# Two layers of a trunk in one launch: weights first at the start, b and k swapped in one head's half, five transposes a pair, samples behind the last chain

## The chip, the cores and the metric

One core of one Trainium2 chip runs the whole program. The metric is the device time of one execution in microseconds (us); a profile of one execution stands beside it.

## The reference

One inference step of a two-layer trunk, model width 1024, over 256 prompt tokens and 8 samples of 4 tokens, 288 columns in all, in float32. Layer 0 mixes tokens with Mamba-2, layer 1 with RWKV-7; around the mixers stand SwiGLU blocks and a gated table product, at the end a norm:

```
for i in range(2):
    h += 0.5 * swiglu(rmsnorm(h), ffn1[i])
    h += mamba2(rmsnorm(h)) if i == 0 else rwkv7(rmsnorm(h))
    h += 0.5 * swiglu(rmsnorm(h), ffn2[i])
    h += (p[i] @ ple_in[i]) * sigmoid(rmsnorm(h) @ ple_gate[i])
y = rmsnorm(h)
```

The change concerns RWKV-7 above all. For each of 16 heads of 64 features, with r, k, v, decay d, a unit vector kk and a gate a, it carries a 64x64 state:

```
sa = S @ -kk_t
S  = S * d_t + sa (kk_t * a_t)^T + v_t k_t^T
y_t = S @ r_t
```

The prompt starts from zero; each of the 8 samples has a state of its own, which is an output. y is then normalised per head, a bonus sum(r * k * r_k) * v is added, the result is gated and multiplied by w_o.

## The kernel before

Features lie on partitions (eight tiles `h[k]` of 128x288), tokens on the free axis. The stages run in the order above. Weights come as a stream of 512 KB units of eight 128x128 tiles (`Stream.load`, L46, on SyncE's queue). ScalarE copies each half unit into a rounded part `whi` (L61) and VectorE subtracts to get the rest `wlo` (L62); a product is three matmuls of 288 columns (L160, L161, L162).

`start` (L243 to L247) issues the vectors `vec`, two tiles of h, the first weight unit, and six tiles of h, all from SyncE. Meanwhile `prologue` (L441) runs WARM = 16 rounds of matmuls on a constant tile. `final` sums squares over features with six matmuls (L419: three for `ss`, three for `sq`), transposes the result 24 times into token rows (L429), scales each block of 512 columns by the norm on ScalarE or VectorE (L434) and stores it (L435).

The RWKV stage takes heads in pairs: `p` counts eight of them, and the two heads of a pair are the two halves of the 128 partitions. Per pair there are these parts:

- `bulk` and `bulk2`: the projections, matmuls of 128x288. They are the filler that a loop weaves in between the others, RATE = 1.6 of its steps for each round of the chains.
- `prep` (from L1260): the decay E1, its inverse E2, and the tiles `AR` (kk and r, scaled) and `BK` (b = kk times a in slot 0, k in slot 1, both times E2), each holding four chunks of 64 prompt tokens and one with the samples. `pad_mul` (L1255 the chunks, L1257 the samples) writes them on VectorE. `by_tokens` multiplies BK with AR (masked into `AA`, L1313 and L1322) and, against an identity, turns BK into `BKt` with tokens on partitions; all of it is L1307. After it comes a triangular inverse by small matmuls (L1352).
- `chain` (from L1410): chunk by chunk `solve` (L1435 to L1444), `solved` (L1449, L1450) and `state` (L1461 to L1469); in chunk 2 the samples: `masked` builds `SVm` (L1479), `samples` multiplies (L1486, L1489), updates the sample states `S0` on VectorE (L1491, L1492) and stores them. Then center (L1233 and L1234, a matrix that subtracts the mean), squares, `ones_m` for the variance, and the gated output.
- `wo`: the output products, filler of the last pairs. EARLY output tiles are taken in hand one round sooner; TAIL tells how many steps fill each round behind the last chain.

A scheduler sets the order on each engine; only in the tail the order written is kept (`k.keep`).

## Time and profile before

| What | Value |
| --- | --- |
| Runs | 1524.62, 1524.87, 1526.18 us; median 1524.87 |
| Profiled execution | 1526.08 us, span 1524.3 us |
| Busy TensorE, VectorE, ScalarE, GpSimd | 1503.7, 1107.9, 971.8, 62.0 us |
| RWKV, head pairs | about 1000 to 1260 us |
| One head pair in the middle | 30.6 us, TensorE busy 30.41 |
| First real matmul | at 7.90 us |

The profile is of one execution. Times are in microseconds, PE is TensorE (PEld its weight load), DVE VectorE, ACT ScalarE, POOL GpSimd, SP SyncE; a q behind the name is the engine's queue. L12 is line 12 of the kernel before. A group row gives busy time, mean ns of one, and the idle time ahead of the engine with what ended it; a row of the timeline gives start, length, and in brackets that idle time.

### The profile page before, as it was taken

What the parts mean: (1) busy time and instruction counts of PE and PEld (TensorE: products, weight loads), DVE (VectorE), ACT (ScalarE), POOL (GpSimd) and SP (SyncE); (2) the same over time, 40 slices, a digit from 0 to 9 for tenths busy, and PEclk for the clock granted to TensorE, in tenths of its full rate; (3) what the DMA queues carried; (4) which work ended last, traced back from release to release, by engine and by line L of the source; (5) the groups of instructions that cost most, each with busy time, mean ns of one, the idle gap of its engine ahead of it and who ended that gap; (6) DMA issues with size and microseconds to landing.
All of it is one profiled execution on the core that took longest, in us unless ns stands there. A gap on an engine that the chain in (4) does not pass through costs nothing.

```text
span 1524.3 us, 35699 instructions
## 1 busy us (share of the span) xinstructions
PE 1503.7 (99%) x14210; PEld 1425.9 (94%) x14210; DVE 1107.9 (73%) x2336; ACT 971.8 (64%) x2217; POOL 62.0 (4%) x162
## 2 busy tenths in 40 slices
PE   9999999999999999999999999999999999999997
PEld 9999999999999999999999999778887779999997
DVE  7666568899998766656866655898888768666566
ACT  6555458999997655554755554687767646555545
POOL 0000002112110000000000000300000000000000
PEclk9999999999999999999999999999999999999999
DMA  7555564766766555555555555612222225555552
GB/s 232 166 166 167 167 203 141 236 237 217 235 224 192 180 167 166 166 166 167 161 168 166 167 167 166 207 69 73 85 72 83 74 66 169 167 167 166 166 169 67
DMA packets 75575, 243.48 MB, mean 160 GB/s; under 512 B 11728, under 2 KB 16976, under 8 KB 75408
## 3 DMA queue, kind: packets, MB, share of 16 engines
q1 hardware_dynamic: 75408, 241.21, 50.2%
q8 instruction: 111, 1.82, 0.5%
q14 instruction: 56, 0.46, 0.1%
HBM read 226.54 MB, written 14.64 MB: 158 GB/s over the span
## 4 chain that ended last, share of the span: by engine, by line
PE 90%; DVE 4%; ACT 3%; DMA 1%; issue 1%; SPq 0%; DVEq 0%; ACTq 0%
PE bank L160 25%; PE bank L162 25%; PE bank L161 25%; PE bank L1352 2%; PE bank L1307 1%; PE bank L785 1%; DVE wlo L62 1%; PE bank L1172 1%; PE bank L789 1%; PE bank L781 1%; PE bank L1489 1%; PE bank L1461 1%; PE bank L1449 1%; PE bank L1421 1%; DMA raw<-in_w 1%
## 5 line engine op out<-in xcount | busy, mean ns | idle before, releaser
L160 PE MATMUL bank<-act,whi 128*128 128x288 f32 x2792 | 833.5, 299 | 2.3 <-ACT whi L61 0.8
L161 PE MATMUL bank<-act,whi 128*128 128x288 f32 x2792 | 828.8, 297 | 0.0
L162 PE MATMUL bank<-act,wlo 128*128 128x288 f32 x2792 | 824.7, 296 | 0.1
L61 ACT ACTIVATE whi<-raw 128x512 fp32r<-128x512 f32 x762 | 478.3, 632 | 438.1 <-PE bank L161 425.5
L62 DVE TENSOR_TENSOR wlo<-raw,whi 128x512 fp32r<-128x512 f32 x762 | 521.5, 690 | 269.8 <-ACT whi L61 241.3
L162 PEld LDWEIGHTS bank<-act,wlo 128*128 128x128 f32 x2792 | 527.6, 189 | 5.0 <-issue 2.4
L161 PEld LDWEIGHTS bank<-act,whi 128*128 128x128 f32 x2792 | 528.5, 189 | 3.7 <-DVE act L172 0.3
L160 PEld LDWEIGHTS bank<-act,whi 128*128 128x128 f32 x2792 | 524.1, 188 | 7.8 <-ACT whi L61 1.3
L160 PE MATMUL bank<-more,whi 128*128 128x288 f32 x192 | 56.7, 296 | 0.0
L337 DVE TENSOR_TENSOR u<-bank,s 128x288 f32<-128x288 f32 x88 | 40.2, 457 | 22.8 <-PE bank L162 22.8
L161 PE MATMUL bank<-more,whi 128*128 128x288 f32 x192 | 56.5, 294 | 0.0
L162 PE MATMUL bank<-more,wlo 128*128 128x288 f32 x192 | 56.4, 294 | 0.0
L334 DVE TENSOR_TENSOR t<-bank,rstd 128x288 f32<-128x288 f32 x88 | 39.8, 457 | 22.5 <-PE bank L162 22.5
L686 DVE SCALAR_TENSOR_TENSOR conv_a<-X,vec,conv_a 128x312 f32<-128x312 f32 x96 | 51.1, 536 | 2.4 <-ACT conv_a L145 2.1
L145 ACT ACTIVATE s<-t 128x288 f32<-128x288 f32 x104 | 45.7, 443 | 6.1 <-DVE t L379 4.4
L145 ACT ACTIVATE act<-h,vec 128x288 fp32r<-128x288 f32 (+1 forms) x71 | 37.1, 527 | 4.3 <-DMA h<-in_xT 3.0
L145 ACT ACTIVATE X<-bank 128x256 f32<-128x256 f32 (+2 forms) x98 | 30.3, 339 | 13.8 <-PE bank L1352 13.4
L161 PEld LDWEIGHTS bank<-more,whi 128*128 128x128 f32 x192 | 36.3, 189 | 0.0
L162 PEld LDWEIGHTS bank<-more,wlo 128*128 128x128 f32 x192 | 36.3, 189 | 0.0
L160 PEld LDWEIGHTS bank<-more,whi 128*128 128x128 f32 x192 | 36.0, 187 | 0.0
L140 ACT ACT_TABLE_LOAD x25 | 32.1, 1283 | 1.1 <-PEq L1789 0.7
L172 DVE SCALAR_TENSOR_TENSOR act<-h,vec,act 128x288 fp32r<-128x288 f32 x56 | 28.4, 513 | 5.8 <-ACT act L145 5.8
(390 smaller groups left out, 1730.9 us busy)
## 6 DMA issues: line engine op xcount, KB each, us to landing
raw<-in_w SPq DMA_DIRECT2D x381, 512.0 KB, 3.6
h0a<-in_ssm_a SPq DMA_DIRECT2D x16, 512.0 KB, 5.5
h0b<-in_ssm_b SPq DMA_DIRECT2D x16, 512.0 KB, 5.0
out_ssm_s<-h0b SPq DMA_DIRECT2D x16, 512.0 KB, 4.2
AA<-in_wn SPq DMA_DIRECT2D x6, 512.0 KB, 4.4
S<-in_wkv_in SPq DMA_DIRECT2D x8, 256.0 KB, 3.8
out_wkv_s<-S SPq DMA_DIRECT2D x8, 256.0 KB, 2.0
h<-in_xT SPq DMA_DIRECT2D x8, 144.0 KB, 4.6
```

The costliest lines, as they stand in the source:

```text
L61: nc.scalar.activation(hi, src, AF.Copy)
L62: nc.vector.tensor_tensor(lo, src, hi.bitcast(F32), ALU.subtract)
L140: load = self.nc.scalar.preload_act_table_set(s)
L145: i = self.nc.scalar.activation(out, in_, func, **kw)
L160: self.keep(self.nc.tensor.matmul(ps, wh, xh, start=start, stop=False))
L161: self.keep(self.nc.tensor.matmul(ps, wh, xl, start=False, stop=False))
L162: self.keep(self.nc.tensor.matmul(ps, wl, xh, start=False, stop=stop))
L172: nc.vector.scalar_tensor_tensor(lo, src, scale, hi.bitcast(F32), ALU.mult, ALU.subtract)
L334: nc.vector.tensor_tensor(t, pg, r, ALU.mult)
L337: nc.vector.tensor_tensor(u, pu, s, ALU.mult)
L686: nc.vector.scalar_tensor_tensor(a[:, :312], X[:, t:t + 312], k.g(f"conv_w{t}")[:, ct:ct + 1], a[:, :312], ALU.mult, ALU.add)
L1352: k.keep(nc.tensor.matmul(ps[rows, ch], lhs(ch)[rows], rhs(ch)[rows], start=True, stop=True))
```

## The change

The warm-up has 10 rounds in place of 16. The first weight unit comes as two halves, ahead of everything on SyncE's queue; h0, `vec`, h2 and h4 are issued from ScalarE, the other h tiles from SyncE between weight units. In `final` the transposes of the last block stand behind the sums, and the last two stores are issued from ScalarE. EARLY and TAIL change in one number each. In the lower head's half (h = 1) of `BK`, b and k change places, so that one 128x128 transpose of a chunk gives both heads' rows; five of these replace the 20 matmuls against the identity. k times E2 is written by GpSimd, kk times E2 by VectorE in two halves. `SVm` is one instruction, and for the last pair the sample update (L1516 after) stands behind the center products.

```diff
-WARM = 16
+WARM = 10
...
+    def load_first(self):
+        t = self.pool.tile([P, UT * P], F32, tag="raw", name="raw0", bufs=self.bufs)
...
+        for o in range(0, UT * P, PT * P):
+            self.k.nc.sync.dma_start(t[:, o:o + PT * P], self.dram[0][:, o:o + PT * P])
+            yield
...
-        nc.sync.dma_start(self.vec, io["vec"])
-        for k in range(KD):
-            nc.sync.dma_start(self.h[k], io["xT"][:, k])
-            if k == 1:
+        first = self.ws.load_first()
+        nc.scalar.dma_start(self.h[0], io["xT"][:, 0])
+        next(first)
+        nc.scalar.dma_start(self.vec, io["vec"])
+        next(first)
+        for k in range(1, KD):
+            (nc.scalar if k in (2, 4) else nc.sync).dma_start(self.h[k], io["xT"][:, k])
+            if k % 2 == 1 and k < KD - 1:
                 self.ws.load()
...
-                nc.tensor.transpose(pt[:, P * j:P * j + P], self.y[4 * half + j][:, o:o + P], self.I)
+                t = nc.tensor.transpose(pt[:, P * j:P * j + P], self.y[4 * half + j][:, o:o + P], self.I)
+                if c == 2:
+                    self.after(t, total)
...
-            nc.sync.dma_start(self.io["y"][o + lo:o + P, q], out[c][lo:, q])
+            (nc.sync if i < 4 else nc.scalar).dma_start(self.io["y"][o + lo:o + P, q], out[c][lo:, q])
...
-EARLY = 2
-TAIL = 4, 4, 4, 10
+EARLY = 1
+TAIL = 4, 2, 4, 10
...
+        self.I128 = self.t("I128", [P, P])
+        nc.gpsimd.memset(self.I128, 0.0)
+        for h in range(2):
+            q = slice(64 * h, 64 * h + 64)
+            nc.gpsimd.tensor_copy(self.I128[q, q], self.I[q])
...
-        self.pad_mul(BK[:, :, 1], k2, E2)
+        for h, rows, _ in H:
+            self.pad_mul(BK[rows, :, h], k2[rows], E2[rows], eng=nc.gpsimd)
...
-        self.pad_mul(BK[:, :, 0], kk, E2)
+        for h, rows, _ in H:
+            self.pad_mul(BK[rows, :, 1 - h], kk[rows], E2[rows])
...
-        by_tokens(ps, 4, 320, 64, lambda rows: AR[rows, 4, 0])
+        by_tokens(ps, 4, 384, 64, lambda rows: AR[rows, 4, 0])
         for ch in range(5):
-            by_tokens(ps, ch, 64 * ch, 64, lambda rows: self.I[rows])
+            o = P * (ch % 2 if ch < 4 else 2)
+            k.keep(nc.tensor.transpose(ps[ch // 2 % 2][:, o:o + P], BK[:, ch].rearrange("p i t -> p (i t)"), self.I128))
...
-        for h in range(2):
-            k.act(BKt[:, h], ps[h][:, :320].rearrange("p (c t) -> p c t", c=5), AF.Copy)
+        for i in range(2):
+            k.act(BKt[:, :, 2 * i:2 * i + 2].rearrange("p h c t -> p c h t"),
+                  ps[i][:, 0:256].rearrange("p (c h t) -> p c h t", c=2, h=2), AF.Copy)
+        k.act(BKt[:, :, 4], ps[0][:, 256:384].rearrange("p (h t) -> p h t", h=2), AF.Copy)
...
                 if ch == 2 and n == 2:
-                    samples()
+                    samples_y()
+                    if p < KD - 1:
+                        samples(k.bank("R"))
...
         self.square(pc, sh, sl, k.tmp("sq"))
+        if p == KD - 1:
+            samples(k.bank("main"))
```

In the rows of order a name stands as out<-in with a buffer's number behind it; line numbers of the changed kernel lie 9 to 31 higher. Across the program TensorE has 12334 rows where it had 12428, VectorE 2280 for 2289, ScalarE 2102 for 2090, GpSimd 200 for 166.

ScalarE at the start of the program, before (`act` is the first product's input, `whi` a weight part):

```order
L140 ACT_TABLE_LOAD
L145 ACTIVATE act_17_81<-h_2_73,vec_129 128x288
L145 ACTIVATE ss_204<-h_2_73 128x288
L145 ACTIVATE act_19_83<-h_4_74,vec_129 128x288
L145 ACTIVATE sq_206<-h_4_74 128x288
L61 ACTIVATE whi_172<-raw_137 128x512
L145 ACTIVATE act_21_85<-h_6_75,vec_129 128x288
```

And now:

```order
L253 DMA h_2_73<-in_xT 128x288
L255 DMA vec_129<-in_vec 128x370
L258 DMA h_6_75<-in_xT 128x288
L258 DMA h_10_77<-in_xT 128x288
L149 ACT_TABLE_LOAD
L154 ACTIVATE act_17_81<-h_2_73,vec_129 128x288
L70 ACTIVATE whi_167<-raw_135 128x512
L154 ACTIVATE act_19_83<-h_4_74,vec_129 128x288
```

Four transfers are issued ahead of the table load, the first weight part follows the first input directly, and the two squares in front of it have gone behind.

TensorE in a middle head pair, before (`r_const` holds the identity):

```order
L1352 MATMUL bank_2131_17935<-XT_2114_17845,Z_17890 64x64
L1449 MATMUL bank_2145_18038<-rhs_17993,TT_17597 64x64
L1449 MATMUL bank_2146_18039<-rhs_17993,TT_17597 64x64
L1118 MATMUL bank_2212_18338<-lg_1226_13464,whi_17705 128x288
L1119 MATMUL bank_2212_18338<-lg_1226_13464,wlo_17706 128x288
L1307 MATMUL bank_2133_17946<-AR_1264_13630,BK_13632 64x64 x2
L1307 MATMUL bank_2133_17946<-r_const_13601,BK_13632 64x64 x10
L1352 LDWEIGHTS N_2019_17373
```

And now:

```order
L1329 MATMUL bank_2009_17240<-AR_1264_13628,BK_13631 64x64
L1344 MATMUL bank_2009_17240<-I_1255_13599,BK_13631 128x128 x2
L1461 MATMUL bank_2010_17267<-S_17213,AR_1265_13629 64x64 x2
L1463 MATMUL bank_2010_17267<-SAV_16788,AA_15927 64x64 x2
L1467 MATMUL bank_1969_17049<-AR_1265_13629,S_17213 64x64 x2
L1459 MATMUL bank_2012_17276<-r_const_13596,q_17066 64x64 x2
L1463 MATMUL bank_2012_17276<-SAV_16788,AA_15927 64x64 x2
L1329 MATMUL bank_2008_17239<-AR_1264_13628,BK_13631 64x64 x2
L1344 MATMUL bank_2008_17239<-I_1255_13599,BK_13631 128x128 x3
```

Here `I_1255` is the 128x128 identity. The ten identity matmuls in each of two banks have become two and three transposes; they stand between matmuls of 64x64.

TensorE at the end of the last chain, before:

```order
L1489 MATMUL bank_2339_18932<-SVm_18891,BKt_17893 64x512
L1489 MATMUL bank_2339_18932<-SVm_18892,BKt_17893 64x512
L1435 MATMUL bank_2341_18948<-S_18928,AR_1264_13630 64x64 x2
L1437 MATMUL bank_2341_18948<-SAV_18534,AA_17892 64x64 x2
L1441 MATMUL bank_2305_18754<-AR_1264_13630,S_18928 64x64 x2
L1449 MATMUL bank_2343_18960<-rhs_18955,TT_18634 64x64
L1449 MATMUL bank_2344_18961<-rhs_18955,TT_18634 64x64
L1461 MATMUL bank_2346_18980<-SAV_18534,BKt_17893 64x64 x2
L1469 MATMUL bank_2305_18754<-AA_17892,SAV_18534 64x64 x2
L1233 MATMUL bank_2351_19015<-ch_18991,center_13612 128x288
L1234 MATMUL bank_2351_19015<-cl_18992,center_13612 128x288
```

And now:

```order
L1461 MATMUL bank_2332_18819<-S_18801,AR_1265_13629 64x64 x2
L1463 MATMUL bank_2332_18819<-SAV_18441,AA_17815 64x64 x2
L1467 MATMUL bank_2298_18633<-AR_1265_13629,S_18801 64x64 x2
L1475 MATMUL bank_2334_18833<-rhs_18826,TT_18539 64x64
L1475 MATMUL bank_2335_18834<-rhs_18826,TT_18539 64x64
L1487 MATMUL bank_2337_18847<-SAV_18441,BKt_17816 64x64 x2
L1495 MATMUL bank_2298_18633<-AA_17815,SAV_18441 64x64 x2
L1253 MATMUL bank_2342_18886<-ch_18862,center_13611 128x288
L1254 MATMUL bank_2342_18886<-cl_18863,center_13611 128x288
L1516 MATMUL bank_2346_18895<-SVm_18766,BKt_17816 64x512 x2
```

The sample products have moved from ahead of the last chunk to behind the center products. Of the 186 output-projection matmuls that stand around this chain, 62 stood ahead of its start, 46 between start and center, 12 from there to the variance products and 66 behind; now they are 72, 18, 6 and 90.

## The prediction

> **What bounds the kernel now.** I read the page's busy times and chain first, then stage windows, the timeline of the start, the RWKV stage and the end, and last the rows of single lines.

> ```profile
> PE 1503.7 (99%) x14210; PEld 1425.9 (94%) x14210; DVE 1107.9 (73%) x2336; ACT 971.8 (64%) x2217; POOL 62.0 (4%) x162
> ...
> PE 90%; DVE 4%; ACT 3%; DMA 1%; issue 1%; SPq 0%; DVEq 0%; ACTq 0%
> ```

> TensorE (PE) is the bound: 99% busy, and 90% of the chain. Outside the places below, only fewer or shorter matmuls can pay. Stage windows (columns: length, then busy PE, PEld, DVE, ACT, POOL, granted clock, DMA share, GB/s) show where that is not so:

> ```profile
> 1127.25:1157.86 30.61, 30.41 (x498) 24.46 (x497) 24.76 (x68) 21.91 (x62) 0.00 (x0) 1.00 0.22 71
> 1157.86:1188.46 30.60, 30.41 (x499) 24.45 (x498) 25.89 (x70) 23.39 (x66) 0.00 (x0) 1.00 0.27 86
> 1255.00:1260.00 5.00, 3.01 (x40) 1.62 (x40) 4.57 (x11) 0.78 (x3) 0.00 (x0) 0.99 0.25 76
> 1260.00:1265.00 5.00, 4.44 (x23) 3.98 (x22) 1.26 (x4) 1.27 (x5) 0.00 (x0) 0.50 0.25 91
> 1265.00:1270.00 5.00, 5.00 (x34) 5.00 (x34) 3.26 (x7) 3.27 (x6) 0.00 (x0) 0.83 0.30 105
> ```

> The first two are one head pair each in the steady RWKV loop: PE is idle 0.20 of 30.6 us, DVE 5.85 and 4.71. The last three are the last pair's chain: PE idle 1.99 of 5 us behind a DVE 4.57 busy, and then a clock of 0.50. The sum is made against the profiled execution, 1526.08 us (span 1524.3), which is 1.21 above the median 1524.87; the forecast is stated from the median.

> **Start.** Before, the first real matmul starts at 7.90 us:

> ```profile
> 1.05 6.77 PE L441 MATMUL bank<-ones_d 128*128 128x128 f32 x32 [1.05 <-DVE eps_n L242]
> 2.13 0.44 SPq L46 DMA_DIRECT2D raw<-in_w  x1
> 3.65 0.54 ACT L145 ACTIVATE act<-h,vec 128x288 fp32r<-128x288 f32 x1 [1.64 <-DMA h<-in_xT]
> 7.21 0.63 ACT L61 ACTIVATE whi<-raw 128x512 fp32r<-128x512 f32 x1 [0.43 <-DMA raw<-in_w]
> 7.90 0.40 PE L160 MATMUL bank<-act,whi 128*128 128x288 f32 x1
> 12.16 0.19 PEld L160 LDWEIGHTS bank<-act,whi 128*128 128x128 f32 x1 [1.06 <-ACT whi L61]
> ```

> ACT splits the first weights (0.63) when the unit has landed at 7.21, 5.1 us after its issue. Now two 256 KB halves are SP's first issues, and h0, vec, h2, h4 go out on ACT's queue ahead of its table load. Issued at about 0.75, a half that took half of the 5.1 would land at 3.3; one that took the whole, at 5.8. h0 and vec move the same way: four issues at SP's 0.44 hold ACT 1.8 us, and then comes its 1.28 us table load, so act needs the landing and ACT free at about 3.9. With the order act (0.54), whi (0.63) the first matmul comes at 3.9 + 1.2 = 5.1 at best and 5.8 + 1.2 = 7.0 at worst. The warm-up of 10 ends at 1.05 + 20/32 of 6.77 = 5.3, so the range is 5.3 to 7.0; I take 6.1, the middle, a gain of 1.8. The second and third unit now stand among the h transfers on two queues; the 1.06 us stall at 12.16 may grow by as much or vanish. I book 0.4 of loss for it and the clock: **-1.4** (-2.6 with 5.3 and the stall as it is; +0.9 with 7.0, the stall doubled and 0.7 lost to a slow clock).

> The clock: rows of single lines (min/median/max in ns) and, below them, two of the chain behind the last head pair (start, length).

> ```profile
> L441 PE MATMUL bank<-ones_d x32: 275/421/582, 1.0 to 7.5; 128*128 128x128 f32 x32
> ...
> L429 PE MATMUL bank<-act,act x24: 272/273/309, 1513.1 to 1516.2; 128*128 128x128 f32 x24
> ...
> 1264.40 0.24 PE bank L160
> ...
> 1266.96 0.13 PE bank L160
> ```

> A 128x128 matmul takes 421 ns in the warm-up against 273 late, and a trunk matmul 0.24 against 0.13 where the clock is 0.50. With 16 rounds the rise lay ahead of the first real matmul (7.90). If with 10 it still comes at about 7.2, matmuls from 6.1 on run at half rate for 1.1 us and lose 0.55; if one more half-rate stretch like the tail's (1260.0 to 1266.8) were to follow, it would cost half of that, 3.4. My 0.4 stands between nothing and 0.55.

> [...]

> **Eight pairs.** The rows of both sides (a chain row is start, length, what):

> ```profile
> L1307 PE MATMUL bank<-r_const,BK 64*64 64x64 f32 x320 | 15.4, 222 | 0.0
> ...
> 1139.28 0.33 PE bank L1119
> 1139.61 0.72 PE bank L1307 x19
> ...
> 1155.68 0.14 PE bank L160
> ...
> 1513.22 2.57 PE bank L429 x23
> ```

> Removed: 20 matmuls against the identity a pair, 40 records. In the chain one adds 0.72/19 = 0.038 us, so 1.52 a pair; the busy sum gives 15.4/8 = 1.93 as the upper end. Added: five 128x128 transposes. L429 is this operation: 2.57/23 = 0.112 each, 0.56. They stand in a group of two and one of three amid 64x64 matmuls, and a full-array matmul behind such costs 0.33 where one behind its like costs 0.14: two entries, 0.38 (none if a trunk matmul is beside them, four if leaving costs as much). Net 1.52 - 0.56 - 0.38 = 0.58 a pair, 4.6 for eight; ends 0.20 and 1.37 a pair. ACT copies BKt in three instructions instead of two; ACT is 22 to 23 of 30.6 us busy, so it costs nothing unless the transposes come late. The 128x128 identity is a memset and two copies on POOL, ahead of the first pair; POOL is 4% busy, and if it were late the first transposes would wait for it as for BK.

> The other side is who writes BK:

> ```profile
> L1307 PEld LDWEIGHTS bank<-AR,BK x320: 129/133/136, 1002.7 to 1202.2; 64*64 64x64 f32 x160
> ...
> L1255 DVE TENSOR_TENSOR BK<-k,ss x8: 416/420/427, 1001.1 to 1186.9; 128x256 f32<-128x256 f32 x8
> ...
> L1257 DVE TENSOR_TENSOR BK<-k,ss x8: 181/185/186, 1001.4 to 1188.6; 128x32 f32<-128x32 f32 x8
> ...
> L1049 POOL TENSOR_TENSOR center<-r_const,t 64x64 fp32r<-64x64 f32 x2 | 1.0, 503 | 0.1
> ...
> L671 POOL COPY X<-conv_in x32: 201/461/1490, 223.0 to 432.2; 128x24 f32<-128x24 f32 x32
> ...
> 1199.52 1.07 PE bank L1307 x29
> ```

> k times E2 leaves DVE (0.42 + 0.19 = 0.61 a pair), but kk times E2 is now written in halves, by two instructions where one stood, with the same columns: again 0.61 more. DVE gains nothing. On POOL no such instruction exists: L1049 gives 0.50 for 64 columns; with 0.20 fixed (L671's least) that is 0.0047 a column, so 1.4 for 256 and 0.35 for 32, 3.5 us for both heads; from 1.2 (DVE's rate) to 11.3 (L671's largest over its median, 3.2 times). In the first pair DVE's k part starts at 1001.1 and PE needs it at 1002.7: POOL ends at 1004.6, 1.9 us late if PE has nothing else; I take 1.2, the ends being 0 and 1.9 (or more if POOL is slow). In the last pair the k part starts at 1186.9 and the products at 1199.52, so 3.5 us is hidden there by 12.6; if that cover went, up to 3.5 a pair would be the price. Sum: -4.6 + 1.2 = **-3.4** (-11.0 with 1.37 and no first wait; +0.3 with 0.20 and 1.9).

> **Samples and tail.** In the last chain the sample update stands between chunks two and three:

> ```profile
> 1256.77 1.08 PE L1489 MATMUL bank<-SVm,BKt 128*64 128x512 f32 x4 [0.41 <-DVE bv L1503]
> ...
> 1258.11 0.60 DVE S L1491
> 1258.71 0.14 DVE rhs L1444
> 1258.84 0.60 DVE S L1492
> 1259.47 0.24 DVE SAV L1450
> ```

> Its two DVE steps hold back rhs and SAV: 1.2 us of chain go, and 1.08 of PE moves behind the center matmuls, where PE else waits for the square. Against that the order table has only 18 output-projection matmuls between the chain's start and center, where 46 stood: 28 x 0.13 = 3.7 us of cover that now runs behind it. One SVm instruction of 1024 columns for two of 512 is the same work. With 1.99 idle to win at most: -3.2 (1.2 + 1.99) to +3.7; I take **-1.0**, nearest to the row of the 1.2, since cover that leaves is not idle twice: it only moves where the chain already waits.

> **End.**

> ```profile
> 1514.55 0.44 ACT L145 ACTIVATE sq<-h 128x288 f32<-128x288 f32 x1
> 1515.62 0.73 PE L419 MATMUL bank<-ones_d,sq 128*128 128x1 f32 x6
> ...
> 1517.77 1.97 ACT L145 ACTIVATE out<-bank,rstd 128x512 f32<-128x512 f32 x3 [0.89 <-DVE rstd L195]
> ...
> 1518.48 3.06 SPq L435 DMA_DIRECT2D out_y<-out  x6
> ```

> sq is ready at 1514.99, but its sums wait for all 23 transposes until 1515.62; with 16 ahead (16 x 0.112 from 1513.22: 1515.01) they start 0.6 earlier, and the scale and everything behind follow. The eight transposes left are done (0.9) before the scale, which comes 2.15 behind the start of the sums (1517.77). The six output issues take 0.51 each on SP; two on ACT save up to 1.0 of issue, but ACT issues after its last eviction: I take 0.3. Sum **-0.9** (-0.3 to -1.6).

> All: -1.4 - 3.4 - 1.0 - 0.9 = -6.7, so 1526.08 - 6.7 = 1519.4 for an execution like the profiled one, 1518.2 from the median.

> **Rivals.** [...]

> The pairs give more: 1.93 - 0.56 - 0.38 = 0.99 a pair is 7.9 for eight; with POOL's first wait hidden that is 4.5 more than the 3.4 of the sum, so 1513.7. For it speaks the busy sum, against it that those durations overlap.

> The change doesn't do what it says in the pairs: the PE time freed there turns into waits for DVE, whose work is not less; then 0 for the pairs: 1521.6. Against it: PE idles only 0.20 us a pair now.

> Tail bare of cover: +3.7 in place of -1.0 gives 1522.9. For it: the clock of 0.50 just behind the idle stretch; more idle, longer half rate.

> Slower: POOL and DVE hold each other up in every pair. L671, one shape, takes 201 to 1490 ns beside a busy DVE. If one POOL multiply's length, 1.4 us a pair, arrives on PE by way of late DVE steps of the chain, the total goes up by 8 x 1.4 = 11.2: 1529.4. It undoes the sum from 6.7/8 = 0.83 us a pair on. Against it: DVE's idle 4.7 us a pair would take in 3.5.
> [...]

> **How the numbers follow.** Chances: the forecast 0.46, cold start 0.12, pairs give more 0.10, pairs give nothing 0.12, bare tail 0.10, slower 0.10. The range 1513.5 to 1523.0 takes in the forecast and all rivals but the slower one; a tenth or so of their strays falls outside. 0.2% is 3.05 us, about what a measurement of this kernel can tell from no change: faster is below 1521.82, slower above 1527.92. The case at 1521.6 sits on that edge and is halved: faster 0.46 + 0.12 + 0.10 + 0.06 = 0.74; same 0.06 + 0.10 = 0.16; slower 0.10, the last case.

> **What would show it.** Start: first real matmul near 6.1, with 128x288 spacing 0.13 from there. Pairs: a pair of 30.0 us instead of 30.6, PE still above 29.8 busy, transposes 0.11 apart, POOL instructions near 1.4 us. Tail: no sample step between rhs and SAV; the stretch from the last chain's start to center shorter, granted clock there not lower for longer. End: sums of sq at 16 transposes, last output issue 0.6 to 1.2 earlier. Wrong it would be by POOL instructions over 3 us, by DVE over 29 us busy in a pair, or by PE idle over 3 us around the last chain.

## The result, and the profile after

The changed kernel takes 1541.94 us (median, 1540.43 to 1546.53) against 1525.17 in the runs beside it: a ratio of 1.0111, 95% interval 1.0091 to 1.0130. It is 16.8 us slower; the forecast was 6.7 faster. The profiled execution took 1541.16 us, its span 1539.4.

The page after, busy times, the slices of the granted clock, and the chain:

```profile
PE 1515.6 (98%) x13918; PEld 1427.7 (93%) x13918; DVE 1109.8 (72%) x2327; ACT 971.9 (63%) x2225; POOL 81.7 (5%) x197
...
PEclk9999999999999999999999999999999978999999
...
PE 90%; DVE 4%; ACT 3%; issue 1%; DMA 1%; DVEq 0%; ACTq 0%
```

PE has 292 instructions fewer and is busy 11.9 us longer. Two slices of the clock row, which stood at 9 throughout before, are 7 and 8. Stage windows (columns as in the prediction), first a head pair in the middle, then three stretches around the last chain:

```profile
1141.35:1173.79 32.44, 31.90 (x464) 24.78 (x463) 24.90 (x67) 22.40 (x63) 1.86 (x4) 1.00 0.22 67
1227.42:1237.66 10.24, 9.93 (x109) 7.90 (x111) 4.90 (x14) 4.66 (x12) 0.00 (x0) 0.50 0.01 3
1237.66:1254.72 17.06, 15.77 (x170) 11.74 (x166) 9.59 (x25) 5.91 (x17) 0.00 (x0) 1.00 0.26 80
1254.72:1278.62 23.90, 20.32 (x140) 14.45 (x141) 12.58 (x32) 7.34 (x20) 0.00 (x0) 0.50 0.09 25
```

Two losses show. A pair takes 32.44 us where it took 30.61, with 464 matmul records for 498, PE still busy and the clock full. And around the last chain 34 us run at half rate in two stretches, where before it was 6.8 (1260.0 to 1266.8). The half-rate stretches of the change are 10.24 and 23.90 us long and the one between them 17.06, so 3, 7 and 5 times 3.413; the stretch at full rate behind them, 1278.62 to 1534.62, is 75 times that. Before, the half-rate stretch is 6.83 (1259.92 to 1266.74, twice 3.413) and the one at full rate behind it 252.59, 74 times. So in the later part of these two traces the clock changes only at the ends of windows of that length.

Cut at the first product of the last pair (BK by AR, the first matmuls that need BK), the two traces give what each loss is worth. From the first product of the first pair to there it is 194.6 us before (1002.7 to 1197.3) and 202.0 in the change (1001.1 to 1203.1), both at full clock: 7.4 us go to longer pairs. From there to the end it is 327.0 and 336.3, so 9.3 us more, and there lie the half-rate stretches. The start gives 1.6 back.

The start came as drawn: the first real matmul at 6.67, full rate from there, without the 1.06 us stall.

```profile
1.05 4.58 PE L456 MATMUL bank<-ones_d 128*128 128x128 f32 x20 [1.05 <-DVE eps_n L251]
...
5.56 0.53 ACT L154 ACTIVATE act<-h,vec 128x288 fp32r<-128x288 f32 x1 [1.65 <-DMA vec<-in_vec]
6.00 0.61 ACT L70 ACTIVATE whi<-raw 128x512 fp32r<-128x512 f32 x1
...
6.67 0.40 PE L169 MATMUL bank<-act,whi 128*128 128x288 f32 x1 [1.03 <-ACT whi L70]
```

### The profile page after: what moved, and what is told of

It is laid out like the page before. It is cut to its first block, busy times and chain, and to the rows that moved or that the text cites. A ratio compares the mean times of both kernels' runs of the same rounds, so it can differ in the third digit from the quotient of the medians.

```text
span 1539.4 us, 35213 instructions
## 1 busy us (share of the span) xinstructions
PE 1515.6 (98%) x13918; PEld 1427.7 (93%) x13918; DVE 1109.8 (72%) x2327; ACT 971.9 (63%) x2225; POOL 81.7 (5%) x197
## 4 chain that ended last, share of the span: by engine, by line
PE 90%; DVE 4%; ACT 3%; issue 1%; DMA 1%; DVEq 0%; ACTq 0%
PE bank L169 25%; PE bank L171 25%; PE bank L170 25%; PE bank L1378 2%; PE bank L1329 1%; PE bank L800 1%; PE bank L1516 1%; PE bank L1475 1%; DVE wlo L71 1%; PE bank L804 1%; PE bank L796 1%; PE bank L1487 1%; PE bank L1192 1%; PE bank L1253 1%; ACT L149 1%
## 5 line engine op out<-in xcount | busy, mean ns | idle before, releaser
L169 PEld LDWEIGHTS bank<-act,whi 128*128 128x128 f32 x2792 | 524.8, 188 | 10.7 <-issue 1.6
L154 ACT ACTIVATE X<-bank 128x256 f32<-128x256 f32 (+2 forms) x98 | 30.5, 341 | 13.9 <-PE bank L1378 13.7
```

What stands on the lines that cost most here:

```text
L154: i = self.nc.scalar.activation(out, in_, func, **kw)
L169: self.keep(self.nc.tensor.matmul(ps, wh, xh, start=start, stop=False))
```

## The experiments

Times are medians, ratios against the kernel before in the runs beside, with 95% intervals. The last column is the mean granted clock over all runs of that kernel.

| Run | What | us | ratio | clock |
| --- | --- | --- | --- | --- |
| - | before (in the batches) | 1524.8 to 1525.5 | 1 | 0.996 to 0.997 |
| - | the change | 1541.94 | 1.0111 [1.0091, 1.0130] | 0.987 |
| e1 | change, k on DVE | 1546.56 | 1.0153 [1.0119, 1.0186] | 0.983 |
| e2 | change, products in fours | 1543.98 | 1.0127 [1.0112, 1.0142] | 0.987 |
| e3 | change, EARLY and TAIL back | 1536.00 | 1.0085 [1.0064, 1.0105] | 0.990 |
| e4 | before + start, end | 1523.79 | 0.9997 [0.9987, 1.0006] | 0.996 |
| e5 | change, no pair part | 1529.96 | 1.0036 [1.0022, 1.0050] | 0.991 |
| e6 | before + pair part | 1535.02 | 1.0064 [1.0042, 1.0086] | 0.992 |
| e7 | change, no pair part, tail back | 1525.33 | 1.0004 [0.9991, 1.0016] | 0.995 |
| e8 | before + EARLY, TAIL | 1529.77 | 1.0022 [1.0008, 1.0036] | 0.994 |
| e9 | change + 48 matmuls | 1549.32 | 1.0155 [1.0125, 1.0185] | 0.987 |
| e10 | e4 with EARLY 4 | 1524.75 | 1.0000 [0.9985, 1.0015] | 0.996 |
| e11 | e4 with EARLY 3 | 1521.29 | 0.9970 [0.9958, 0.9982] | 0.998 |
| e12 | before + k on POOL | 1525.68 | 0.9999 [0.9986, 1.0011] | 0.997 |
| e14 | change, identity matmuls | 1528.70 | 1.0029 [1.0014, 1.0044] | 0.989 |
| e15 | change, EARLY 3 | 1535.88 | 1.0075 [1.0056, 1.0094] | 0.992 |
| e16 | e7 with EARLY 3 | 1523.28 | 0.9991 [0.9982, 1.0001] | 0.996 |
| e17 | e14 with EARLY 3 | 1519.04 | 0.9960 [0.9949, 0.9972] | 0.997 |
| e18 | e17, samples in the chain | 1520.79 | 0.9976 [0.9963, 0.9988] | 0.995 |

### First theories: POOL's late k part, and the bare tail

e1 and e2 ask whether POOL, by coming late, is what makes a pair longer.

```diff
 e1:
-            self.pad_mul(BK[rows, :, h], k2[rows], E2[rows], eng=nc.gpsimd)
+            self.pad_mul(BK[rows, :, h], k2[rows], E2[rows])
 e2, in by_tokens (m is each product, i = 1 the k rows):
+                    if i:
+                        last = m
+                    else:
+                        k.after(m, last)
```

> The changed kernel with k times E2 written by DVE again, in halves, as kk times E2 is. Theory A: POOL's late k part makes the scheduler emit the products BK by AR in two groups, so that only two 64x64 quarters of the array work at a time, and breaks up the filler between; the pairs then lost about 7 of the 16 us. A expects about 1534.5, with head pairs 30.6 or less apart and the AR products of a pair taking 1.8 us of PE instead of 2.7; the half-rate stretches around the last chain remain. Rival B: the pairs are slower because transposes and 64x64 matmuls alternate, whoever writes BK; B expects pairs still 32.4 apart and 1541. Rival C: everything is the clock behind the last pair; then 1541 with the pairs as they are.

> The changed kernel with POOL still writing k times E2, but each product of the b rows ordered behind the product of the k rows of the same chunk, so that four quarters of the array alternate as before. Theory A (the order is what costs): the same as with k on DVE, about 1534 to 1535, unless the wait for POOL is longer. Rival (POOL and DVE hold each other up): 1540 or more, since POOL's instructions are still there, and DVE instructions beside them longer than 0.42 and 0.69 us.

Theory A fell: e1 took 1546.56 and e2 1543.98, where it expected 1534.5. e2 did put many of the products back in fours, which shortens them (2.73 us of PE in a pair for 3.46), but its middle pairs are still 32.4 apart. POOL was innocent in the profile too; the rows of the multiplies after, and DVE's own beside them:

```profile
L1275 POOL TENSOR_TENSOR BK<-k,ss x16: 715/736/1239, 999.4 to 1187.2; 64x256 f32<-64x256 f32 x16
L1275 DVE TENSOR_TENSOR BK<-rs_q,ss x16: 405/418/423, 1003.4 to 1204.5; 64x256 f32<-64x256 f32 x16
L1275 DVE TENSOR_TENSOR AR<-r,E x8: 414/416/426, 998.4 to 1195.6; 128x256 f32<-128x256 f32 x8
```

0.74 us against the estimate of 1.4, and DVE's multiplies as long as before (0.42). e12, the kernel before with only this step moved, settles it:

```diff
...
-        self.pad_mul(BK[:, :, 1], k2, E2)
+        self.pad_mul(BK[:, :, 1], k2, E2, eng=nc.gpsimd)
```

> The kernel before with k times E2 written by POOL and nothing else: no swap, no transposes, all 20 identity matmuls. If the transposes cost the pairs their time (theory P), this is 1524 to 1526 with pairs 30.6 apart; if POOL costs it, by its late k part or by holding DVE up, it is 1530 or more and the AR products of a pair take 2.4 us as in the kernel with the pair part alone.

1525.68, ratio 0.9999: in the kernel before, POOL costs nothing that can be measured.

e3 puts EARLY and TAIL back; e8 is that part alone.

```diff
 e3:                              e8:
-EARLY = 1                       -EARLY = 2
-TAIL = 4, 2, 4, 10              -TAIL = 4, 4, 4, 10
+EARLY = 2                       +EARLY = 1
+TAIL = 4, 4, 4, 10              +TAIL = 4, 2, 4, 10
```

> The changed kernel with EARLY 2 and TAIL 4, 4, 4, 10 as before, so more output products lie between the start of the last chain and its center. Theory T: bare chains let the clock fall to half; with 44 in place of 27 fillers there the second half-rate stretch (24 us long) shrinks to some 10 and the time falls by about 7, to 1535. Rival: the fall of the clock comes from late small matmuls ahead of the last chain (it falls first at 1227, still within the last prep), and EARLY and TAIL change nothing: 1540 to 1542.

> The kernel before with only EARLY 1 and TAIL 4, 2, 4, 10: 30 instead of 46 output-product matmuls between the last chain's start and center. Theory of the clock: the array streams for less than about a third of a 3.41 us window there, the clock falls to half for longer than before's 6.8 us; each such window costs up to 1.7 us: 1527 to 1531. If fillers only move behind the chain without the clock, at most 16 x 0.13 = 2 us: 1525 to 1527.

Both agree with the theory of the tail: 6 us come back in the change, and 5 are lost in the kernel before, with a lower mean clock (0.990 for 0.987, 0.994 for 0.997). But 11 us of the change remain.

### The parts alone and undone

e4 takes over `load_first`, `start`, WARM and `final` as the front's diff shows them; e6 the pair part (pad_mul, BK's places, I128, transposes, BKt); e5 is the change without the pair part; e7 is e5 with EARLY and TAIL as in e3.

```diff
 e5, e7 (against the change):
-            k.keep(nc.tensor.transpose(ps[ch // 2 % 2][:, o:o + P], BK[:, ch].rearrange("p i t -> p (i t)"), self.I128))
+            by_tokens(ps, ch, 64 * ch, 64, lambda rows: self.I[rows])
...
-            self.pad_mul(BK[rows, :, h], k2[rows], E2[rows], eng=nc.gpsimd)
+        self.pad_mul(BK[:, :, 1], k2, E2)
```

> The kernel before with only the start and the final part of the change. The trace of the change shows the first real matmul at 6.67 instead of 7.90 and the first pair 1.1 us earlier, and the end, from the first sums to the last instruction, 0.25 shorter: 1525.2 - 1.4 = about 1523.8. If the start's gain were lost again before the first pair, it would be 1525.

> The kernel before with only the pair part (b and k swapped, transposes, k times E2 on POOL, BKt in three copies). Theory P expects pairs 32.4 apart, +7 by the last pair, and, since there is less matmul work in a window of 3.41 us, half-rate windows ahead of the last chain: 1533 to 1537. If only EARLY, TAIL and samples brought the loss, the pairs keep 30.6 and it is 1522 to 1525.

> The changed kernel without the pair part: BK, the multiplies and the 20 identity matmuls a pair as before; start, end, SVm, samples, EARLY and TAIL as changed. Theory P: in the pairs the five transposes need the whole array, while the 64x64 identity matmuls filled quarters that the AR products left free, so the pairs lost 1.9 us each although 40 matmul records went; with them back the pairs are 30.6 apart and the last pair starts at 1196 instead of 1203. P expects 1526 to 1530, what is above 1523.8 being half-rate windows around the last chain. Rival R: EARLY, TAIL and the samples alone make the clock fall; then over 1533.

> The changed kernel without the pair part and with EARLY and TAIL of before: start, end, SVm in one and the last sample update behind the center remain. Both theories expect it at or below the kernel with the ends alone (1523.8): about 1522 to 1524. Over 1527 would mean that the moved sample update itself costs.

e4 and e5 came as expected; e7, at 1525.33, lies 1.3 above its range. e6 has the time that was expected, but not the pairs: in its trace they are 30.9 apart and not 32.4. The times of the parts nearly add up: ends -1.1 (e4), pair part +10.2 (e6), EARLY and TAIL +5.0 (e8) are +14.1 of the 16.8. The moved samples are e7 against e4, +1.5, within the intervals of both.

e14 undoes the transposes only, and keeps swap, halves and POOL:

```diff
-        by_tokens(ps, 4, 384, 64, lambda rows: AR[rows, 4, 0])
+        by_tokens(ps, 4, 320, 64, lambda rows: AR[rows, 4, 0])
...
-            k.keep(nc.tensor.transpose(ps[ch // 2 % 2][:, o:o + P], BK[:, ch].rearrange("p i t -> p (i t)"), self.I128))
+            by_tokens(ps, ch, 64 * ch, 64, lambda rows: self.I[rows])
```

> The changed kernel with the 20 identity matmuls a pair instead of the five transposes, and all else kept: swap, halves, POOL, tail, samples, ends. Theory P: the transposes are what the pairs lose by; pairs 30.6 to 31.2 apart, AR products 1.1 to 1.5 us of PE a pair, and the time that of the kernel without the pair part, 1528 to 1532. Rival (the swap and POOL's late k part order the products in twos): 1536 to 1542.

1528.70, 13 us less than the change, and its pairs are even shorter than before, 29.6 where 30.6 to 31.2 were expected. The lines that the transposes share with the AR products, in one pair each; the first two rows are the change (AR products, then transposes), the third is e14 (products and identity matmuls); columns PE, PEld, clock, DMA share, GB/s:

```profile
1141.35:1173.79 32.44, 3.46 (x40) 2.57 (x40) 1.00 0.22 67
1141.35:1173.79 32.44, 0.98 (x5) 0.51 (x5) 1.00 0.22 67
```

```profile
1139.10:1168.70 29.60, 3.33 (x80) 2.83 (x80) 1.00 0.30 92
```

The 80 records take 3.33 us, the 45 that replace them 4.44. The chain of the pair in the change:

```profile
1139.84 1.01 PE bank L1329 x14
1140.85 0.33 PE bank L169
...
1141.71 0.67 PE bank L1329 x10
...
1142.64 0.20 PE bank L1329 x3
1142.84 0.37 PE bank L1344 x2
```

Before, one piece of 29 records took 1.07 (the row of 1199.52 in the prediction has the same length); now 14 take 1.01. In their rows a product stands as 64*64, a quarter of the 128*128 of a trunk matmul or a transpose. In the trace before, most products of a pair start in fours, 0.11 us from four to four, and the identity matmuls start among the last of them. In the change the products start in twos from the first one on, also 0.11 from two to two, so two go in the time of four. Two transposes, each of the whole 128*128, go for 0.37 behind the products, where 0.112 was the price of one behind its like.

How this and the rest make up a pair shows when the time from each matmul's start to the next one's is added up by groups, over one middle pair of each trace:

| Kernel | AR products | identity matmuls or transposes | 72 projection matmuls | 4 sample products | rest | pair |
| --- | --- | --- | --- | --- | --- | --- |
| before | 1.1 | 1.8 | 12.0 | 2.0 | 13.7 | 30.6 |
| the change | 2.8 | 0.8 | 13.2 | 2.0 | 13.7 | 32.4 |
| e2 | 2.6 | 0.8 | 13.7 | 1.0 | 14.4 | 32.4 |
| e6 | 2.6 | 0.8 | 12.7 | 1.0 | 13.6 | 30.9 |
| e14 | 1.2 | 1.6 | 12.1 | 1.0 | 13.7 | 29.6 |

In the change the products alone take as long as products and identity matmuls together did before (2.8 for 2.9), so what went saved 0.1 us; the transposes then cost 0.8, and the projections 1.2. PE enters a whole-array matmul 22 times in a pair, for 18 before; at the 0.33 for 0.14 of the prediction's rows that is 0.8 of the 1.2. The twos alone are not the cause: e2 has many of the products in fours, and its projections take longer still. Why an entry costs more, no run isolates.

The column of the sample products is another matter. They are four records of 512 columns, and in some places the two heads' run side by side, in others one behind the other. Before, the change, e6 and e14:

```profile
1127.25:1157.86 30.61, 2.10 (x4) 0.39 (x4) 1.00 0.22 71
1141.35:1173.79 32.44, 2.10 (x4) 0.39 (x4) 1.00 0.22 67
1139.40:1170.27 30.87, 1.13 (x4) 0.31 (x4) 1.00 0.28 85
1139.10:1168.70 29.60, 1.13 (x4) 0.31 (x4) 1.00 0.30 92
```

This follows from the order that the scheduler set, and no edit aimed at it. It is why e14's pairs are shorter than before, and 1.0 of the 1.5 us by which e6's are shorter than the change's; without it the pair part would make e6's middle pairs about 1.2 us longer than before, not 0.3. So about 1.0 of the 2.8 us between the pairs of the change and of e14 is not the transposes' doing.

### The clock

The pair part alone cost 10.2 us, but its longer pairs only a part. Here the runs of one program speak: e6's nine runs have spans from 1526.5 to 1539.7, and granted clocks from 0.996 to 0.985 in the same order. At 0.996, the clock of the kernel before, e6 takes 1528.6 and 1529.6 us, 4 to 5 more than before; what its median has on top of that, 5 to 6, comes with a lower clock (0.992 in the mean).

e9 was to lift directly the stretches in which the array has little to do:

```diff
...
+                if p >= KD - 2:
+                    pw = k.bank("main")[:, :256]
+                    for _ in range(2):
+                        m = nc.tensor.matmul(pw, self.ones_m, self.warm, start=True, stop=True)
+                        k.after(m, k.last_mm)
...
```

> The changed kernel with 48 matmuls of 128x256 added whose result nothing reads, two in each of 24 rounds of the last two chains, tied behind the chain's own matmuls. Theory of the clock: they bring the thin windows above the point at which the clock falls, and the half-rate time of about 34 to 40 us shrinks to less than half: although 48 x 0.12 = 5.8 us of matmuls are added, the time falls to 1530 to 1536. Rival (the tail is long because its steps wait for each other at any clock, and the half rate is only a sign of it): 1542 to 1548.

It missed: 1549.32, 7.4 more than the change, somewhat over the length of the added matmuls, at the same mean clock. They stood where the chain's rounds put them; the clock fell elsewhere (in its trace first at 1210.6, ahead of the last chain), and the half-rate stretches come to 31 us for 34. Whether matmuls without use could hold it in a better place stays open.

e13 measures the clock by itself, in a section behind the program, in one execution:

```diff
...
+        for n in (8, 6, 5, 4, 3, 2):
+            full(60)
+            for _ in range(int(24 / (0.9 + 0.13 * n))):
+                ps = k.bank("main")
+                for _ in range(n):
+                    mm(ps[:, :NT], W, X)
...
+                nc.vector.tensor_scalar(X, ps[:, :NT], 0.0, 1.0 / 128.0, ALU.mult, ALU.add)
...
+                    mm(ps[i % 2][o, :P], one[r, :64], one[r, :P])
...
+            t = nc.tensor.transpose(ps[:, :P], one[:, :P], k.I)
```

> The kernel before with a section behind its end that writes no output: ten stretches of some 24 us, each behind 60 full matmuls of 128x288 (8 us). Six of groups of 8, 6, 5, 4, 3, 2 such matmuls, each group waiting for a DVE instruction on the result of the one ahead; then 64x64 matmuls of 128 columns back to back on one, two and four quarters of the array; then 210 transposes of 128x128. Theory S (the clock falls where matmuls stream for less than about 0.35 of a 3.41 us window, counted by area of the array): full clock at 8 and 6 a group, half at 3 and 2; half on one quarter (0.25 of the area), full on four. Theory U (any matmul in flight counts): only the gaps matter, and one quarter back to back keeps the full clock. The transposes: full clock if they count like matmuls; half within 3.4 us if they do not. The time itself has no meaning here; about 350 us longer.

Windows of its section: groups of 8, 6, 5 (two rows: ahead of the fall and behind), 4, 3 and 2 (likewise), then one quarter, two, four, and the transposes:

```profile
1533.30:1553.90 20.60, 14.57 (x88) 11.99 (x88) 5.04 (x11) 0.00 (x0) 0.00 (x0) 1.00 0.01 1
1563.40:1584.40 21.00, 13.84 (x78) 10.78 (x78) 5.95 (x13) 0.00 (x0) 0.00 (x0) 1.00 0.00 1
1593.80:1604.10 10.30, 6.50 (x35) 4.86 (x35) 3.20 (x7) 0.00 (x0) 0.00 (x0) 1.00 0.01 2
1604.10:1619.00 14.90, 10.99 (x36) 8.57 (x36) 3.21 (x7) 0.00 (x0) 0.00 (x0) 0.50 0.00 0
1630.80:1634.20 3.40, 2.29 (x12) 1.68 (x12) 0.92 (x2) 0.00 (x0) 0.00 (x0) 1.00 0.00 0
1634.80:1657.40 22.60, 15.97 (x49) 11.80 (x49) 5.49 (x12) 0.00 (x0) 0.00 (x0) 0.50 0.00 1
1668.70:1672.30 3.60, 1.96 (x9) 1.28 (x9) 1.37 (x3) 0.00 (x0) 0.00 (x0) 1.00 0.00 0
1672.30:1695.30 23.00, 15.29 (x43) 10.43 (x43) 6.41 (x14) 0.00 (x0) 0.00 (x0) 0.50 0.00 1
1706.30:1709.70 3.40, 1.75 (x7) 1.06 (x8) 1.37 (x3) 0.00 (x0) 0.00 (x0) 1.00 0.00 0
1709.90:1731.60 21.70, 12.93 (x32) 7.56 (x30) 7.33 (x16) 0.00 (x0) 0.00 (x0) 0.50 0.00 0
1742.30:1766.90 24.60, 24.60 (x225) 24.41 (x224) 0.00 (x0) 0.00 (x0) 0.00 (x0) 1.00 0.00 1
1775.20:1799.80 24.60, 24.60 (x449) 24.55 (x448) 0.00 (x0) 0.00 (x0) 0.00 (x0) 1.00 0.01 3
1808.10:1832.90 24.80, 24.80 (x897) 24.56 (x896) 0.00 (x0) 0.00 (x0) 0.00 (x0) 1.00 0.02 5
1841.10:1863.90 22.80, 22.80 (x211) 22.80 (x210) 0.00 (x0) 0.00 (x0) 0.00 (x0) 1.00 0.00 1
```

Streaming is counted here by starts: 128x288 matmuls back to back start 0.13 us apart at full clock (the chain row of 1266.96 in the prediction). PE's busy time is longer, 0.93 us for a group of five in the rows below. A group of n takes n x 0.13 of streaming in a period of 20.6/11 = 1.87 us for 8, 21.0/13 = 1.62 for 6, 10.3/7 = 1.47 for 5. The clock held at a share of 6 x 0.13/1.62 = 0.48, fell after 10 us at 5 x 0.13/1.47 = 0.44, and within 4 us with groups of 4, 3 and 2 (3.40, 3.60 and 3.40 us at 1.00 ahead of the fall), though PE shows as busy in 63% of such a stretch (6.50 of 10.30) and idles 0.55 us between its groups:

```profile
1598.23 0.93 PE L1755 MATMUL bank<-X,W 128*128 128x288 f32 x5 [0.55 <-DVE X L1779]
...
1608.39 1.57 PE L1755 MATMUL bank<-X,W 128*128 128x288 f32 x5 [0.55 <-DVE X L1779]
```

Those 10 us are three windows of 3.41. As the groups fall into them, they hold shares of 0.49, 0.46 and 0.38 (estimates from the starts, at 0.13 a matmul), and the clock fell at the end of the third: by this estimate it held behind a window of 0.46 and fell behind one of 0.38, in one execution.

Once fallen it stayed: the same five take 1.57 and their period is 2.12, a share of 5 x 0.24/2.12 = 0.57 (0.24 apart at 0.50), and the clock was 0.50 to the end of that stretch (1604.10 to 1619.00); behind the next 60 full matmuls it was 1.00 again (1630.80). By area, theory S was wrong: one quarter back to back kept a clock of 1.00 for 24.6 us, and transposes for 22.8. Theory U was wrong too, since the gaps are 0.55 with six a group, where the clock held (7.16 of 21.00 us for 13), and 0.55 with five, where it fell. What goes with the clock in these rows is the share of time in which any matmul streams. One quarter, two and four also take the same time, 24.6, 24.6 and 24.8 us for 225, 449 and 897 records: matmuls on different quarters ran side by side.

The transposes stood alone for those 22.8 us, so here they held a clock that was up. Whether they would raise one that has fallen was not run.

The kernel's tail fits this. The groups of PE in the window of 3.41 us ahead of the first fall in the change (1224.00 to 1227.42):

```profile
L1447 PE MATMUL bank<-AR,S 64*64 64x8 f32 x32 | 1.1, 200 | 0.0
L1378 PE MATMUL bank<-X,N 64*64 64x64 f16 x16 | 0.8, 196 | 0.0
...
L1378 PE MATMUL bank<-Z,XT 64*64 64x64 f16 x8 | 0.3, 198 | 0.0
L1378 PE MATMUL bank<-XT,Z 64*64 64x64 f16 x8 | 0.3, 193 | 0.0
```

Of its 68 matmuls 32 have eight columns and 32 are 64x64 in f16; the other four, left out here, are 288 wide. By their columns, at the 0.13 us for 288 (0.45 ns a column; for f32 records of other widths 0.85, as the 24.6 us for 225 records of 128 in e13 give), and with those that run side by side counted once, they stream for about a third of the window (an estimate). The ones that lay ahead of each fall in e1 to e12 come to between 0.16 and 0.53 by the same estimate, most below 0.42. The windows that kept the clock agree, by the same estimate: from 1000 us to the end of the last chain the lowest of them is at 0.42 before and 0.44 in the change, where the falls came behind 0.41 before, and 0.34 and 0.18 in the change. Some of the other traces have falls and no falls mixed between 0.36 and 0.53, so the estimate doesn't settle every window. Several windows of the RWKV stage lie not far above the shares that stood ahead of falls (eight from 0.42 to 0.52 before, by the estimate), so a little less matmul work, or the same work in other places, could bring some of them there. Nor do the clock's changes keep to a fixed time from the program's start: with the changed start the clock first rises at anything from 4.0 to 10.7 us in the traces. Whether this is why one program spreads over 13 us is not shown.

### Filler in the other direction, and a faster kernel

e10, e11, e15 and e16 set EARLY to 4 or 3 with TAIL of before; e17 is e14 with that, e18 has the samples back in the chain.

```diff
 e11 (e10: 4), on e4:        e15 to e18:
-EARLY = 2                   -EARLY = 1
+EARLY = 3                   -TAIL = 4, 2, 4, 10
                             +EARLY = 3
                             +TAIL = 4, 4, 4, 10
 e18 also:
-                    if p < KD - 1:
-                        samples(k.bank("R"))
+                    samples(k.bank("R"))
```

> The kernel before with the start and the final part of the change and EARLY 4: the change of EARLY in the other direction, 72 instead of 46 output-product matmuls between the last chain's start and center. Theory of the clock: the last chain keeps the full clock; against 1523.8 with EARLY 2, 2 to 4 us less: 1520 to 1522, and below before by more than 2. Rival: fillers there only make the chain longer: 1524 or more.

> The same with EARLY 3: 64 output-product matmuls in the chain. Theory of the clock: between 1520 and 1523.8. Rival: 1524 or more.

> The changed kernel with EARLY 3 and TAIL 4, 4, 4, 10: 51 output-product matmuls in the last chain where it has 18 and e3 has some 40. Theory of the clock: below e3's 1536, at 1530 to 1534. Rival: 1536 or more, since the first fall comes ahead of the last chain, in the last prep, where EARLY changes nothing.

> The changed kernel without the pair part, with EARLY 3 and TAIL of before: start, end, SVm and moved samples with the filler of e11, which took 1521.3. If the moved samples help where the chain is covered, 1519 to 1521; by e7 against e4 they cost 1.5, which would give 1522 to 1523.

> The changed kernel with the 20 identity matmuls in place of the transposes, EARLY 3 and TAIL 4, 4, 4, 10; swap, halves, POOL, ends and moved samples stay. By the theory (transposes and thin windows were the two losses): e14's pairs, 29.6 apart, and e11's or e16's filler: 1517 to 1522. If shorter pairs only mean thinner windows, the clock takes it back: 1524 to 1530.

> The same with the last sample update in the chain again, as in e11. By e11 against e16 (1521.3 and 1523.3) 1 to 2 us below e17: 1516 to 1521. If the place of the samples does not matter, as e17.

EARLY 3 gives e11 1521.29, at a clock of 0.998; EARLY 4 gives nothing (1524.75, a miss for the 1520 to 1522 expected), so more filler is not better without end. In the change it brought no more than EARLY 2 (1535.88 against e3's 1536.00): a miss, the falls ahead of the last chain are left, as the rival said. e17, all of the change but the transposes, with EARLY 3, is the fastest here: 1519.04, ratio 0.9960 [0.9949, 0.9972]. Its last chain and its pairs, for comparison with the windows above:

```profile
1134.50:1164.10 29.60, 29.45 (x500) 24.16 (x499) 25.82 (x67) 21.96 (x62) 2.83 (x4) 1.00 0.30 91
1193.20:1256.00 62.80, 60.85 (x911) 48.09 (x910) 44.92 (x119) 31.68 (x88) 0.00 (x0) 1.00 0.25 78
1256.00:1262.00 6.00, 6.00 (x29) 4.77 (x30) 3.07 (x6) 2.40 (x6) 0.00 (x0) 0.72 0.28 102
```

One window of half rate is left there. Against e16, which has the same filler, ends and samples but not swap, halves and POOL, e17 is 4.2 us faster. Of the 1.0 us that a middle pair is shorter (29.6 for 30.6), the sample products, side by side in all pairs of e17 and in four of e16's eight, give 0.95; so this gain too is an order that was found, not work that was removed. e18 was expected below e17 and came out 1.7 above; the intervals overlap, so the place of the samples stays open.

## Why the prediction was wrong, point by point

- **Eight pairs, -3.4: the step that failed first.** "In the chain one adds 0.72/19 = 0.038 us, so 1.52 a pair" took the records' cost as what their absence would save. From start to start they do take 1.8 us; but the AR products, which had run among them, take 2.8 without them instead of 1.1, so 0.1 was saved and not 1.52. The transposes cost 0.8 for the 0.56 booked, and the projections' entries 1.2 for 0.38. A middle pair went from 30.6 to 32.4, outside the bounds given (0.20 to 1.37 saved), and the pairs together lost 7.4 us where 4.6 were to be won.
- **POOL, +1.2 for the first pair:** too high; 0.74 instead of 1.4 us a multiply, and e12 is equal to before. The slower rival, POOL and DVE holding each other up, was the wrong mechanism for the right sign.
- **Tail, -1.0: the other failed step.** The clock of 0.50 was quoted, and priced only as a stretch at the start and as 3.7 of moved cover in the rival "tail bare". That rival had the right mechanism at too low a price. The half rate went from 6.8 to 34 us, and the stretch from the last pair's first product to the end is 9.3 us longer. EARLY and TAIL alone cost 5.0 (e8), and of the pair part's 10.2 (e6) 5 to 6 come with a lower clock (0.992 for 0.997): that fewer small matmuls in the pairs would cost clock was no term at all.
- **Start, -1.4 and end, -0.9:** the first matmul at 6.67 for 6.1, inside 5.3 to 7.0; the clock rose in time, and the cold start did not come in the profiled run. In e4's trace one window did run at half rate there:

```profile
7.40:10.80 3.40, 3.40 (x16) 3.40 (x15) 3.40 (x8) 3.38 (x8) 0.00 (x0) 0.50 0.94 350
```

  It is no exception. In 7 of the 15 traces with this start (e1, e4, e10, e11, e14, e15, e18) the trunk matmuls from 7.4 to 9.9 us start 0.24 apart and not 0.13; in none of the five with the old start do they. So a cold start, 0.12 among the chances, is real in about half of the executions, at some 1.7 us each (an estimate: half of the 3.40 at 0.50 in the row), where 0.4 was booked; the change's own profile was lucky there.

  In the change the sums started with 16 transposes ahead, and from the first sums to the end it is 11.7 us for 11.9:

```profile
1528.43 2.04 PE L442 MATMUL bank<-act,act 128*128 128x128 f32 x16
...
1530.40 0.83 PE L432 MATMUL bank<-ones_d,sq 128*128 128x1 f32 x6
...
1533.36 1.81 SPq L450 DMA_DIRECT2D out_y<-out  x4
1534.65 1.10 ACTq L450 DMA_DIRECT2D out_y<-out  x2
```

  Together they give 1.1 (e4), half of what was booked, and not told from nothing by its interval.
- **The form of the argument:** nearly every term was a sum of durations at full clock. PE busy at 99% was read as "the array works". By columns it streams for about 0.7 of a middle pair before, and for 0.5 from the last pair's first product on to the end of its chain in the change (estimates, as above), and in e13 the clock held at a share of 0.48 and fell at 0.44.

## What to carry to other kernels

PE busy in a profile is not matmul work: in e13 63% busy was a streaming share of 0.44, and the clock fell. Before removing or gathering small matmuls, count by columns how much streams in each window between which the clock changes (3.41 us here), and compare it with the shares at which the clock was seen to hold and to fall (0.48 and 0.44 in e13). Here 4.6 us were to be won in the pairs, and 5 to 6 of what the pair part lost came with a lower clock (e6). The identity matmuls, which ran side by side with others, saved much less than their records cost when they went, 0.1 us a pair and not 1.52, and the transposes put among 64x64 matmuls cost 0.8 a pair, where 0.56 is their price behind their like. When a change carries several parts, run each alone, and look at one stage of each trace besides the total: one EARLY more was worth 2.5 here (e11 against e4), the loss lay in the transposes and in EARLY and TAIL as changed, and 1.0 us a pair came and went with the scheduler's order for four matmuls that no part was about.
